# A seven-product decoder step: first quarter summed in PSUM, the last recurrent chain later, the gate product on DVE

## The chip, the cores and the metric

One core of a Trainium2 chip runs the whole program. The metric is the device time of one execution in microseconds; the median of several runs counts.

## What is computed

One layer of a hybrid decoder for a prompt of 2048 rows of 1024 numbers and 8 sample rows, in float32. Cut to what matters here:

```python
h = rmsnorm(x) * (1 + scale) + shift
q, k, v, ga, xr, gr, ma, mr = split(h @ w_in)
o  = windowed_attention(q, k, v)
ya = o * silu(ga)
xc = causal_conv(xr)                      # width 4
hs = rglru(xc)                            # h[t] = a[t] * h[t-1] + u[t]
yr = hs * silu(gr)
merged = sigmoid(ma) * (ya @ w_pa) + sigmoid(mr) * (yr @ w_pr)
y = x + gate * (merged @ w_out)
```

Beside y, the last keys, values, convolution rows and recurrent states go out.

## The kernel before

The prompt is worked in two halves of 1024 rows. Each half has its keys, values and attention first, and then a long line of 218 *slots*. A slot is twelve matmuls of 128x512 on PE: for each of four pieces of 128 rows the product of the high parts, and two with a low part (float32 is split in two fp32r numbers, "high" and "low", by a cast on ACT and a subtraction on DVE, S<-B,S or B<-B,B in the views). A matmul of this form takes about 0.23 us, a slot 2.8 us.

Most of the line is made of *Fast* units: a 256x1024 piece of an output as 2x2 quarters by seven products instead of eight (a scheme of Strassen's kind), each product one slot. Weights are loaded, added to each other and split some slots ahead. The products sum in two PSUM banks, X (tiles pg, from a pool of three) and Y (tiles pq, two). Product 0 belongs to quarter (0,0) and to all the others; so after it ACT copies bank X to SBUF (`keep`), and after product 1, which has bank Y to itself, DVE adds the two (`add`) and the quarter goes to the unit's own `evac`. Products 2 to 6 go on in the banks; two units run in turns (`pair`), so that between product 0 and product 1 of a unit there is a slot of the other unit. There are 26 Fast units per half.

What an engine does beside a slot is entered with `line.on(slot, rank, fn)`. Within a slot the ranks are issued in order: EVAC, SIDE, SPLIT, FORM, CHAIN, LATE, STORE, LOAD. Every engine works in the order of this program; nothing is reordered. All instructions carry the line of one helper (L60), so the views are read by tiles: S and B are SBUF tiles, pg, pq and pt PSUM banks, M small tiles, H middle ones, HC the state of the recurrence.

The slots of a half, in order:

- 0 to 17: first merge and attention gates.
- 18 to 129: four times `rnn(p)` (a pair of Fast units for xr and gr), each followed by a pair of gate units. The recurrent *chain* of `rnn(p)` (convolution, gate matmuls into pt, exps on ACT, a product `drive` on POOL, the scan on DVE, a product `out` on POOL, and its store) is entered at slots c(i,j). For p = 3, c(1,0) and c(1,1) are 124 and 127, so its scans stand in slots 137 and 138, its POOL products in 136 to 139.
- 130 to 157: `pa`, the attention projection, two pairs of Fast units. ACT adds 1 to the loaded merge gate (`plus`), and for three of the four quarters POOL multiplies it by the quarter (after DVE's add); the fourth is one scalar_tensor_tensor on DVE.
- 158 to 189: `pr`, the recurrent projection. Its operand is yr, which came through memory (yrd): `load_split` loads a chunk on SP, and ACT and DVE split it three slots later. In the second half eleven small stores of the final states (`state_out`, to out_dram) go through SP's queue near there.
- 190 to 217: the output projection; merged comes back from memory (mgd).

In the first half `phase_h` prepares the rows of the second one beside the pa and pr slots: loads, a root mean square per row (squares on ACT, the small M operations on POOL, the scaling on DVE), transposes on PE.

Of the kernel before, what the change touches and what calls it, by code (L numbers as in the profile page):

```python
# [16 lines left out]
ALU = mybir.AluOpType  # L17
# [24 lines left out]
def tile_hybrid_step(ctx: ExitStack, tc: tile.TileContext, x_prompt, x_sample, cache_k, cache_v, state_conv,  # L42
# [189 lines left out]
    onec = C([P, 1], tag="onec")  # L232
    V.memset(onec, 1.0)
# [186 lines left out]
    def phase_h(line, t0):  # L420

        def group(g, t0):
            xts = []
# [15 lines left out]
            for i in range(4):  # L439
                line.on(t0 + 2 * i, LOAD, lambda i=i: load(i))  # L440
                line.on(t0 + 4 + 2 * i, CHAIN, lambda i=i: rms_rows(xts[i], P))
# [608 lines left out]
    EVAC, SIDE, SPLIT, FORM, CHAIN, LATE, STORE, LOAD = range(8)  # L1050
# [83 lines left out]
    class Fast:  # L1134
# [18 lines left out]
        def mm(self, n):  # L1153
            wn, xn, bn = PROD[n]
            if n in (0, 1, 3):
                self.bank[bn] = PG() if bn == "X" else PQ()
            ps = self.bank[bn]
            for k in range(4):
                wh, wl = (t[:, k, :] for t in self.W[wn])
                xh, xl = (self.F[xn][k][:, i, :] for i in range(2))  # L1160
                T_.matmul(ps, wh, xh, start=(n in (0, 1, 3) and k == 0), stop=False, skip_group_check=True)
                T_.matmul(ps, wh, xl, start=False, stop=False, skip_group_check=True)
                T_.matmul(ps, wl, xh, start=False, stop=(k == 3), skip_group_check=True)
# [4 lines left out]
        def place(self, s):  # L1168
# [51 lines left out]
            line.on(s[0] + 1, EVAC, lambda: keep(0, 0, "X"))  # L1220
            line.on(s[1] + 1, EVAC, lambda: add(0, 0, "Y"))
# [54 lines left out]
    def stages(s, hT, hT1=None, side=None):  # L1276
# [142 lines left out]
        def rnn(p):  # L1419
# [185 lines left out]
            c = {(0, 0): t0 + 12, (0, 1): t0 + 15, (1, 0): t0 + 22, (1, 1): t0 + 25}  # L1605
# [98 lines left out]
        def pa(p):  # L1704
# [12 lines left out]
            def plus(i, j):  # L1717
                A.activation(tm[i, j], tm[i, j], AF.Identity, bias=onec)

            def evac(i, j, x, t):  # L1720
                y = tm[i, j]
                if t is None:
                    V.scalar_tensor_tensor(y, y, 1.0, x, op0=ALU.add, op1=ALU.mult)
                else:
                    G_.tensor_tensor(y, y, x, op=ALU.mult)
                    free(t)
                line.after(1 if t is None else 2, STORE, lambda: store(i, j))
# [9 lines left out]
            def loads(t0):  # L1737
                for n, i, j in ((1, 0, 0), (4, 1, 1), (5, 0, 1), (6, 1, 0)):
                    line.on(t0 + 2 * n - 4, LOAD, lambda i=i, j=j: load(i, j))
                    if n < 6:  # L1740
                        line.on(t0 + 2 * n, LATE, lambda i=i, j=j: plus(i, j))
# [11 lines left out]
        for i, (k, c) in enumerate(quarters):  # L1753
            load_split(yrd, yrx, k, c, pa_end - 9 + 7 * i // 8, 3)
# [98 lines left out]
        def out(u):  # L1853
# [12 lines left out]
            def evac(i, j, y, t):  # L1866
                if t is None:
                    t = xt[0] if end else Tt([512])
                    if end:
# [398 lines left out]
```

## Time and profile before

| | |
|---|---|
| median of three runs | 1936.6 us (1935.42 to 1936.63) |
| profiled execution | 1935.09 us, span 1933.4 us |
| PE busy | 1889.7 us, 11000 matmuls |
| DVE, ACT, POOL busy | 1421.6, 1046.9, 541.1 us |
| granted TensorE clock | 0.999 in the mean |
| line of the first half | about 297 to 962 us |
| line of the second half | about 1232 to 1926 us |

PE's busy time is modelled to the end of the pipelined matmuls; what is missing to the span is time in which PE stood. A row of a timeline gives the start in us from the span's begin, the duration, the engine and operation, how many alike follow each other, and in brackets the idle time just before and who ended it.

### The profile page before, as it was taken

How to read it: one execution, taken by the hardware profiler on the slowest of the kernel's cores; microseconds unless marked ns; L12 is line 12 of the kernel's file. 1: busy time of each engine (PE TensorE's matmuls, PEld its weight loads, DVE VectorE, ACT ScalarE, POOL GpSimd, SP SyncE). 2: the span in 40 equal slices, each digit the busy share in tenths (PEclk: the TensorE clock that was granted, in tenths of full speed). 3: DMA queues.
4: the chain of work that ended last, by engine and by line, in shares of the span. 5: the costliest groups of instructions: out<-in, count | busy, mean ns of one | idle time of the engine just before them, and what ended most of it. 6: DMA issues, size and time to landing. Idle time of an engine off the chain costs nothing. (4 is left out here: it accounts for less than half of the span.)

```text
span 1933.4 us, 31848 instructions
## 1 busy us (share of the span) xinstructions
PE 1889.7 (98%) x11000; PEld 1523.5 (79%) x11000; DVE 1421.6 (74%) x2881; ACT 1046.9 (54%) x2285; POOL 541.1 (28%) x606
## 2 busy tenths in 40 slices
PE   7999999999999999999999999999999999999999
PEld 4689887777777877787878898777888787777777
DVE  3657878578988897576735777776889798974754
ACT  4535665365757685533524566454757576942332
POOL 2224443001213222372222444400121131232711
PEclk9999999999999999999999999999999999999999
DMA  9613136445444578897822221443444455777684
GB/s 302 199 61 99 56 106 188 132 140 183 147 140 167 186 243 281 275 247 157 182 54 66 90 71 56 158 132 91 138 138 147 131 174 176 229 247 235 163 189 69
DMA packets 310912, 301.81 MB, mean 156 GB/s; under 512 B 57869, under 2 KB 220925, under 8 KB 310582
## 3 DMA queue, kind: packets, MB, share of 16 engines
q1 hardware_dynamic: 301310, 272.97, 45.4%
q0 software_dynamic: 9440, 26.80, 7.3%
q8 instruction: 87, 1.43, 0.3%
q14 instruction: 75, 0.61, 0.1%
HBM read 207.51 MB, written 102.71 MB: 160 GB/s over the span
## 5 line engine op out<-in xcount | busy, mean ns | idle before, releaser
L60 PE MATMUL pg<-S,B 128*128 128x512 f32 (+1 forms) x3840 | 917.2, 392 | 11.2 <-DVE B L60 9.3
L60 PEld LDWEIGHTS pg<-S,B 128*128 128x128 f32 (+1 forms) x3840 | 702.5, 188 | 180.2 <-DVE B L60 15.3
L60 DVE TENSOR_TENSOR B<-B,B 128x512 fp32r<-128x512 f32 (+1 forms) x756 | 565.9, 772 | 151.6 <-ACT B L60 143.5
L60 PE MATMUL pq<-S,B 128*128 128x512 f32 (+2 forms) x2208 | 482.3, 381 | 5.4 <-DVE B L60 4.9
L60 POOL TENSOR_TENSOR B<-B,B 128x512 f32<-128x512 f32 x184 | 281.7, 1553 | 717.9 <-ACT B L60 268.6
L60 PEld LDWEIGHTS pq<-S,B 128*128 128x128 f32 (+1 forms) x2208 | 369.8, 187 | 98.2 <-DVE B L60 11.5
L60 ACT CAST B<-B 128x512 fp32r<-128x512 f32 x492 | 296.3, 619 | 58.0 <-DVE B L60 33.6
L60 PE MATMUL pg<-B,S 128*128 128x256 f32 (+1 forms) x1704 | 243.8, 298 | 0.0
L60 PEld LDWEIGHTS pg<-B,S 128*128 128x128 f32 x1704 | 217.7, 189 | 17.2 <-issue 9.9
L60 DVE TENSOR_TENSOR S<-B,S 128x512 fp32r<-128x512 f32 x208 | 169.3, 835 | 31.0 <-ACT S L60 30.6
L60 ACT COPY B<-pg 128x512 f32<-128x512 f32 x118 | 69.1, 586 | 163.1 <-PE pg L60 156.7
L60 ACT CAST S<-B 128x512 fp32r<-128x512 f32 x208 | 124.5, 621 | 58.6 <-DVE B L60 20.6
L60 ACT ACTIVATE B<-B,M 128x129 f32<-128x129 f32 x260 | 102.6, 396 | 92.0 <-DVE M L60 85.5
L60 ACT ACTIVATE B<-B 128x512 f32<-128x512 f32 (+1 forms) x166 | 102.8, 629 | 87.0 <-DVE B L60 82.8
L60 POOL TENSOR_TENSOR B<-B,M 128x512 f32<-128x512 f32 x64 | 67.5, 1073 | 99.9 <-DVE M L60 99.9
L60 DVE TENSOR_TENSOR B<-pq,B 128x512 f32<-128x512 f32 x104 | 71.2, 685 | 31.9 <-PE pq L60 31.9
L60 ACT ACTIVATE B<-pg 128x512 f32<-128x512 f32 x76 | 45.1, 594 | 79.6 <-PE pg L60 78.5
L60 POOL TENSOR_TENSOR M<-M,mhalf 128x8 f32<-128x8 f32 (+4 forms) x70 | 83.8, 1197 | 5.8
L60 DVE SCALAR_TENSOR_TENSOR B<-B,VT,B 128x512 f32<-128x512 f32 x96 | 81.4, 848 | 2.3
L60 ACT COPY H<-pt 128x256 f32<-128x256 f32 (+1 forms) x51 | 17.9, 351 | 120.2 <-PE pt L60 120.2
L60 DVE SCALAR_TENSOR_TENSOR B<-B,B 128x512 f32<-128x512 f32 x106 | 78.6, 746 | 0.2
L60 POOL TENSOR_SCALAR M<-M 128x8 f32<-128x8 f32 (+5 forms) x71 | 15.6, 220 | 214.5 <-DVE M L60 208.2
(206 smaller groups left out, 1762.1 us busy)
## 6 DMA issues: line engine op xcount, KB each, us to landing
B<-in_w_in_dram SPq DMA_DIRECT2D x144, 256.0 KB
B<-yad SPq DMA_DIRECT2D x80, 256.0 KB
B<-in_w_in_dram SPq DMA_DIRECT2D x128, 128.0 KB
B<-hd SPq DMA_DIRECT2D x48, 256.0 KB
B<-in_w_out_dram SPq DMA_DIRECT2D x48, 256.0 KB
S<-in_w_ada_dram SPq DMA_DIRECT2D x32, 256.0 KB
hd<-B SPq DMA_DIRECT2D x32, 256.0 KB
yad<-S SPq DMA_DIRECT2D x16, 512.0 KB
```

Of the source, the lines that this page charges most:

```text
L60: ins = fn(*args, **kw)
```

## The change

Six edits:

1. In a Fast unit ACT copies bank X after product 0 into a new bank Y in PSUM (`onto`), one slot after product 0 at a new rank ahead of all others, and product 1 accumulates on it. DVE's `add` of the first quarter is gone; the quarter's `evac` reads the bank. That is 52 copies and 52 adds in the program; where `evac` had an SBUF tile and now has a bank, tanh reads PSUM, and 16 quarters get an ACT copy of their own.
2. In `pa` each quarter's gate product is one scalar_tensor_tensor (add 1, multiply) on DVE: 24 POOL products and 24 ACT `plus` are gone, 24 DVE operations come. The store goes one slot after the evac for all.
3. For p = 3, c(1,0) and c(1,1) are four slots later, 128 and 131, and with them the loads of the gate weights, scans (141, 142), POOL products and stores.
4. `phase_h`: the sum of squares stays where it was, the scaling comes a slot later at rank EVAC (`rms_rows` is these two in one).
5. The yrd chunks are loaded and split two slots earlier.
6. In the output projection of the second half the first quarter's sum takes the way of the others.

```diff
--- before.py
+++ after.py
@@ -229,8 +229,6 @@
     V.tensor_reduce(sel1, ident.rearrange("p (g m) -> p m g", m=32)[:, 8:9, :], op=ALU.add, axis=AX.X)
     V.tensor_tensor(sel1, sel1, ident[:, 9:10], op=ALU.add)
     V.tensor_scalar(sel1, sel1, 0.25, None, op0=ALU.mult)
-    onec = C([P, 1], tag="onec")
-    V.memset(onec, 1.0)
 
     def rstd_of(dst, ss, n, inv):
         G_.tensor_scalar(dst, ss, inv, EPS, op0=ALU.mult, op1=ALU.add)
@@ -420,7 +418,7 @@
     def phase_h(line, t0):
 
         def group(g, t0):
-            xts = []
+            xts, sums = [], {}
 
             def load(i):
                 xts.append([Tt([512]) for _ in range(2)])
@@ -438,7 +436,8 @@
 
             for i in range(4):
                 line.on(t0 + 2 * i, LOAD, lambda i=i: load(i))
-                line.on(t0 + 4 + 2 * i, CHAIN, lambda i=i: rms_rows(xts[i], P))
+                line.on(t0 + 4 + 2 * i, CHAIN, lambda i=i: sums.update({i: rms_sum(xts[i], P)}))
+                line.on(t0 + 5 + 2 * i, EVAC, lambda i=i: rms_scale(xts[i], P, sums.pop(i)))
             for f in range(KT):
                 line.on(t0 + 11 + f, SIDE, lambda f=f: turn(f))
 
@@ -1047,7 +1046,7 @@
 
 
 
-    EVAC, SIDE, SPLIT, FORM, CHAIN, LATE, STORE, LOAD = range(8)
+    ONTO, EVAC, SIDE, SPLIT, FORM, CHAIN, LATE, STORE, LOAD = range(9)
 
     class Line:
         def __init__(self):
@@ -1152,13 +1151,13 @@
 
         def mm(self, n):
             wn, xn, bn = PROD[n]
-            if n in (0, 1, 3):
+            if n in (0, 3):
                 self.bank[bn] = PG() if bn == "X" else PQ()
             ps = self.bank[bn]
             for k in range(4):
                 wh, wl = (t[:, k, :] for t in self.W[wn])
                 xh, xl = (self.F[xn][k][:, i, :] for i in range(2))
-                T_.matmul(ps, wh, xh, start=(n in (0, 1, 3) and k == 0), stop=False, skip_group_check=True)
+                T_.matmul(ps, wh, xh, start=(n in (0, 3) and k == 0), stop=False, skip_group_check=True)
                 T_.matmul(ps, wh, xl, start=False, stop=False, skip_group_check=True)
                 T_.matmul(ps, wl, xh, start=False, stop=(k == 3), skip_group_check=True)
             free(*self.W.pop(wn))
@@ -1217,8 +1216,13 @@
             def last():
                 self.evac(1, 0, bank["X"], None)
 
-            line.on(s[0] + 1, EVAC, lambda: keep(0, 0, "X"))
-            line.on(s[1] + 1, EVAC, lambda: add(0, 0, "Y"))
+            def onto():
+
+                bank["Y"] = PQ()
+                A.copy(bank["Y"], bank["X"])
+
+            line.on(s[0] + (s[1] > s[0] + 1), ONTO, onto)
+            line.on(s[1] + 1, EVAC, lambda: self.evac(0, 0, bank["Y"], None))
             line.on(s[2] + 1, EVAC, lambda: keep(0, 1, "X"))
             line.on(s[3] + 1, EVAC, lambda: keep(1, 1, "Y"))
             line.on(s[4] + 1, EVAC, lambda: add(1, 1, "X"))
@@ -1602,7 +1606,9 @@
             ux = Fast(line, F, in_cols(OFF_XR + 256 * p), xr_evac, sample(hsF, xrS[:, fsl, :], samples_conv))
             ug = Fast(line, F, in_cols(OFF_GR + 256 * p), gr_evac, sample(hsF, grS[:, fsl, :], None))
             t0 = pair(ux, ug)
-            c = {(0, 0): t0 + 12, (0, 1): t0 + 15, (1, 0): t0 + 22, (1, 1): t0 + 25}
+
+            t1 = t0 + (26 if p == 3 else 22)
+            c = {(0, 0): t0 + 12, (0, 1): t0 + 15, (1, 0): t1, (1, 1): t1 + 3}
             for i in range(2):
                 line.on(c[i, 0] - 7, LOAD, lambda i=i: gate_weights(i))
                 line.on(c[i, 0] + 1, SPLIT, lambda i=i: gate_split(i))
@@ -1714,17 +1720,12 @@
                 tm[i, j] = Tt([512])
                 ld.dma_start(tm[i, j], chunk(tmad, 2 * p + i, j))
 
-            def plus(i, j):
-                A.activation(tm[i, j], tm[i, j], AF.Identity, bias=onec)
-
             def evac(i, j, x, t):
                 y = tm[i, j]
-                if t is None:
-                    V.scalar_tensor_tensor(y, y, 1.0, x, op0=ALU.add, op1=ALU.mult)
-                else:
-                    G_.tensor_tensor(y, y, x, op=ALU.mult)
+                V.scalar_tensor_tensor(y, y, 1.0, x, op0=ALU.add, op1=ALU.mult)
+                if t is not None:
                     free(t)
-                line.after(1 if t is None else 2, STORE, lambda: store(i, j))
+                line.after(1, STORE, lambda: store(i, j))
 
             def store(i, j):
                 st.dma_start(chunk(mgd, 2 * p + i, j), tm[i, j])
@@ -1737,8 +1738,6 @@
             def loads(t0):
                 for n, i, j in ((1, 0, 0), (4, 1, 1), (5, 0, 1), (6, 1, 0)):
                     line.on(t0 + 2 * n - 4, LOAD, lambda i=i, j=j: load(i, j))
-                    if n < 6:
-                        line.on(t0 + 2 * n, LATE, lambda i=i, j=j: plus(i, j))
 
             return u, loads
 
@@ -1751,7 +1750,7 @@
         b.final = True
         pa_end = len(seq)
         for i, (k, c) in enumerate(quarters):
-            load_split(yrd, yrx, k, c, pa_end - 9 + 7 * i // 8, 3)
+            load_split(yrd, yrx, k, c, pa_end - 11 + 7 * i // 8, 3)
 
         def pr(f):
             ts = {}
@@ -1865,8 +1864,9 @@
 
             def evac(i, j, y, t):
                 if t is None:
-                    t = xt[0] if end else Tt([512])
-                    if end:
+                    plain = end and (i, j) == (1, 0)
+                    t = xt[0] if plain else Tt([512])
+                    if plain:
                         V.tensor_tensor(t, y, t, op=ALU.add)
                     else:
                         A.copy(t, y)
```

DVE in slots 137 to 140 of the first half before (pg and pq are the banks of the pa units, S and B<-B,B weight splits, HC the scans), and slots 140 to 142 after:

```order
L60 SCALAR_TENSOR_TENSOR B_7830<-B_7786,HC_125,B_7748 128x512
L60 COPY HC_125<-B_7830 128x1
L60 TENSOR_TENSOR B_8071<-B_7637,B_8070 128x512
L60 TENSOR_TENSOR S_8074<-B_7988,S_8074 128x512
L60 SCALAR_TENSOR_TENSOR B_7927<-B_7895,HC_125,B_7868 128x512
L60 COPY HC_125<-B_7927 128x1
L60 TENSOR_TENSOR B_8039<-pg_7796,B_8039 128x512
L60 TENSOR_TENSOR B_8098<-B_7677,B_8097 128x512
L60 TENSOR_TENSOR S_8101<-B_8020,S_8101 128x512
L60 TENSOR_TENSOR S_8104<-B_8022,S_8104 128x512
L60 TENSOR_TENSOR B_8068<-pg_7838,B_8068 128x512
L60 TENSOR_TENSOR B_8139<-B_7634,B_8138 128x512
```

```order
L60 TENSOR_TENSOR B_8028<-pg_7780,B_8028 128x512
L60 SCALAR_TENSOR_TENSOR B_7949<-B_7949,B_8028 128x512
L60 TENSOR_TENSOR B_8099<-B_7598,B_8098 128x512
L60 TENSOR_TENSOR S_8102<-B_8012,S_8102 128x512
L60 TENSOR_TENSOR B_7932<-pq_7951,B_7932 128x512
L60 SCALAR_TENSOR_TENSOR B_7985<-B_7985,B_7932 128x512
L60 TENSOR_TENSOR B_8134<-B_7638,B_8133 128x512
L60 SCALAR_TENSOR_TENSOR B_7913<-B_7877,HC_123,B_7846 128x512
L60 COPY HC_123<-B_7913 128x1
L60 TENSOR_TENSOR B_7964<-pq_7987,B_7964 128x512
L60 SCALAR_TENSOR_TENSOR B_8014<-B_8014,B_7964 128x512
L60 TENSOR_TENSOR B_8156<-B_8072,B_8155 128x512
```

The scans with HC stood ahead of the two pg adds; after the change they stand behind both and between the pq adds, and each of these adds is followed by a SCALAR_TENSOR_TENSOR, the gate product.

POOL over slots 131 to 145 of the first half, before and after (two operands of which the second is an evacuated quarter: a gate product):

```order
L60 TENSOR_TENSOR B_7760<-B_7760,B_7851 128x512
L60 TENSOR_TENSOR B_7794<-B_7794,B_7886 128x512
L60 TENSOR_TENSOR B_7748<-B_7748,B_7746 128x512
L60 TENSOR_TENSOR B_7868<-B_7868,B_7866 128x512
L60 TENSOR_TENSOR B_7830<-B_7830,B_7956 128x512
L60 TENSOR_TENSOR B_7960<-B_7960,B_8039 128x512
L60 TENSOR_TENSOR B_7927<-B_7927,B_7986 128x512
L60 TENSOR_TENSOR B_7990<-B_7990,B_8068 128x512
L60 TENSOR_TENSOR B_8024<-B_8024,B_7974 128x512
L60 TENSOR_TENSOR B_8054<-B_8054,B_8005 128x512
```

```order
L60 TENSOR_TENSOR B_7846<-B_7846,B_7844 128x512
L60 TENSOR_TENSOR B_7944<-B_7944,B_7942 128x512
L60 TENSOR_TENSOR B_7913<-B_7913,B_8038 128x512
L60 TENSOR_TENSOR B_8010<-B_8010,B_8068 128x512
L60 TENSOR_TENSOR M_8424<-M_8424,M_8425 128x1
L60 TENSOR_SCALAR M_8424<-M_8424 128x1
```

Before, the two drives (B_7748, B_7868) and two outs (B_7830, B_7927) of the chain stand among six gate products. After, the drives and outs stand alone, and the M operations of the normalization follow at once.

SP in the second half, around the stores of the final states (out_dram), before and after:

```order
L60 DMA mgd<-B_18843 128x512
L60 DMA B_19046<-yrd 128x512
L60 DMA out_dram<-B_19076 24x128
L60 DMA out_dram<-B_19076 8x128 x9
L60 DMA out_dram<-B_19076 64x128
L60 DMA mgd<-B_18870 128x512
L60 DMA mgd<-B_18898 128x512
L60 DMA B_19099<-yrd 128x512
L60 DMA B_19101<-tmd 128x512
L60 DMA mgd<-B_18926 128x512
L60 DMA B_19128<-yrd 128x512
```

```order
L60 DMA mgd<-B_18800 128x512
L60 DMA B_18973<-yrd 128x512
L60 DMA out_dram<-B_19003 24x128
L60 DMA out_dram<-B_19003 8x128 x9
L60 DMA out_dram<-B_19003 64x128
L60 DMA mgd<-B_18829 128x512
L60 DMA B_19025<-tmd 128x512
L60 DMA mgd<-B_18856 128x512
L60 DMA B_19052<-in_w_proj_rnn_dram 128x4x128
```

Before, two yrd loads are queued behind the eleven stores to out_dram; after, the last yrd load stands ahead of them.

## Rows read from the trace of the kernel before

**Rows 1.** the page's first part: busy us, share, instructions
```profile
PE 1889.7 (98%) x11000; PEld 1523.5 (79%) x11000; DVE 1421.6 (74%) x2881; ACT 1046.9 (54%) x2285; POOL 541.1 (28%) x606
```

**Rows 2.** what PE waited for: us in total, times, longest us
```profile
PE pg L60 <- DVE B L60: 9.3, 11, 2.1
PE pq L60 <- DVE B L60: 4.9, 7, 1.0
...
PE pg L60 <- ACT S L60: 1.6, 1, 1.6
```

**Rows 3.** stretches: length, busy us (instructions) by engine, granted clock, DMA
```profile
300.00:680.00 380.00, 377.16 (x1673) 298.80 (x1672) 311.19 (x473) 229.46 (x393) 76.23 (x55) 1.00 0.51 161
680.00:745.00 65.00, 59.68 (x247) 45.27 (x246) 64.50 (x84) 49.03 (x84) 23.51 (x14) 1.00 0.77 236
745.00:785.00 40.00, 40.00 (x173) 32.03 (x173) 29.06 (x42) 25.07 (x51) 11.65 (x13) 1.00 0.92 305
785.00:796.00 11.00, 8.93 (x35) 6.89 (x33) 9.29 (x16) 3.46 (x8) 3.30 (x7) 0.84 0.79 248
796.00:900.00 104.00, 102.47 (x472) 82.94 (x471) 70.38 (x89) 44.90 (x82) 54.51 (x54) 1.00 0.88 234
...
1638.00:1712.00 74.00, 68.90 (x405) 53.27 (x405) 72.08 (x112) 52.84 (x99) 23.76 (x14) 1.00 0.77 238
...
1760.00:1770.00 10.00, 8.05 (x33) 5.63 (x31) 3.60 (x7) 1.85 (x3) 1.74 (x2) 1.00 1.08 347
```

**Rows 4.** DVE's timeline: start, us, engine, operation, out<-in, count
```profile
729.87 0.69 DVE L60 TENSOR_TENSOR B<-B,B 128x512 fp32r<-128x512 f32 x1
...
734.77 3.49 DVE L60 TENSOR_TENSOR S<-B,S 128x512 fp32r<-128x512 f32 x2
...
742.88 1.18 DVE L60 TENSOR_TENSOR B<-B,B 128x512 fp32r<-128x512 f32 x1
```

**Rows 5.** POOL's timeline beside it
```profile
734.39 3.32 POOL L60 TENSOR_TENSOR B<-B,B 128x512 f32<-128x512 f32 x2 [2.67 <-issue]
...
741.90 1.61 POOL L60 TENSOR_TENSOR B<-B,B 128x512 f32<-128x512 f32 x1 [1.29 <-DVE B L60]
```

**Rows 6.** the page's groups: busy, mean ns, idle before
```profile
L60 ACT COPY B<-pg 128x512 f32<-128x512 f32 x118 | 69.1, 586 | 163.1 <-PE pg L60 156.7
...
L60 DVE TENSOR_TENSOR B<-pq,B 128x512 f32<-128x512 f32 x104 | 71.2, 685 | 31.9 <-PE pq L60 31.9
...
L60 DVE SCALAR_TENSOR_TENSOR B<-B,B 128x512 f32<-128x512 f32 x106 | 78.6, 746 | 0.2
```

**Rows 7.** DVE's timeline before the gap at 789
```profile
784.24 2.39 DVE L60 TENSOR_TENSOR S<-B,S 128x512 fp32r<-128x512 f32 x2
787.35 0.88 DVE L60 TENSOR_SCALAR B<-B,M 128x512 f32<-128x512 f32 x2 [0.72 <-POOL M L60]
```

**Rows 8.** POOL's timeline at that place
```profile
783.86 1.62 POOL L60 TENSOR_TENSOR B<-B,B 128x512 f32<-128x512 f32 x1 [1.29 <-ACT S L60]
```

**Rows 9.** PE's timeline behind that gap
```profile
789.49 4.14 PE L60 MATMUL pg<-S,B 128*128 128x512 f32 x10 [2.07 <-DVE B L60]
...
793.83 2.57 PE L60 MATMUL pg<-S,B 128*128 128x512 f32 x10
```

**Rows 10.** SP's timeline, second half, DMA issues
```profile
1751.09 4.03 SPq L60 DMA_DIRECT2D out_dram<-B  x11
...
1758.79 0.77 SPq L60 DMA_DIRECT2D B<-yrd  x1
```

**Rows 11.** ACT's timeline behind these loads
```profile
1765.41 0.62 ACT L60 CAST S<-B 128x512 fp32r<-128x512 f32 x1 [2.46 <-DMA B<-yrd]
```

**Rows 12.** PE's timeline behind that cast
```profile
1766.08 0.51 PE L60 MATMUL pg<-S,B 128*128 128x512 f32 x1 [1.62 <-ACT S L60]
```

**Rows 13.** ACT and PE around products 0 and 1 of one unit
```profile
887.75 0.59 ACT L60 COPY B<-pg 128x512 f32<-128x512 f32 x1 [7.00 <-PE pg L60]
...
890.34 1.32 PE L60 MATMUL pq<-S,B 128*128 128x512 f32 x5
```

## The prediction

> **What bounds the kernel now.** I read the page's busy shares first. TensorE (PE) works 1889.7 of 1933.4 us [rows 1], so the kernel is a stream of matmuls with only 43.7 us of gaps, and no edit here adds or removes a matmul. Time can only come out of those gaps, or go into new ones. The view of PE's waits then says who ends the gaps: waits for DVE's tiles B, before matmuls into pg and pq, make 14.2 us, and one of 1.6 us is for ACT's S [rows 2]. Last, the table of stretches says where they are [rows 3]. In 680 to 745 us (slots 124 to 143 of the first half) PE stands 65.0 - 59.7 = 5.3 us while DVE is busy 64.5 of 65.0: there DVE is the bound. The same slots of the second half (1638 to 1712) lose 74.0 - 68.9 = 5.1 us, with DVE at 72.1. From 785 to 796 PE stands 2.07 us and its granted clock reads 0.84 instead of 1.00. From 1760 to 1770 it stands 1.95 us. These four places hold 14.4 us. The change touches the work around each of them; elsewhere (300 to 680 for example, 2.8 us in 380) it removes DVE work ahead of gaps before which DVE was not full, and I count nothing.
>
> **Why DVE is late from 680 to 745.** In its timeline an S<-B,S or B<-B,B of 128x512 takes 0.69 us (729.87), but 3.49 for two at 734.77 and 1.18 at 742.88 [rows 4]. Both times POOL runs a 128x512 product: 3.32 us for two from 734.39, and 1.61 from 741.90 [rows 5]. So one product on POOL costs DVE 3.49 / 2 - 0.69 = 1.05 us where DVE asks just after POOL has begun, and 1.18 - 0.69 = 0.5 where it asks later. Of the six gate products on POOL in these slots I find three of the first sort and three of the second: 3 x 1.05 + 3 x 0.5 = 4.7 us of DVE's time per half.
>
> **The change, part by part.**
>
> *Gate product on DVE.* Six POOL products go in each of the two stretches: -4.7 us for DVE. Six scalar_tensor_tensor come; two of them take the place of the add of the first quarter (0.69 us, and the product is 0.75 by its group [rows 6]), so four are new: 4 x 0.75 = +3.0. Net -1.7 us of DVE work per stretch.
>
> *Last chain four slots later.* It removes nothing, but the two scans, the two products before them and the two after them (these four on POOL, at about 1.05 us of DVE each) leave slots 136 to 139, some 2 x 1.28 + 4 x 1.05 = 6.8 us of DVE's time, and land in 140 to 143. Behind those, from 745 to 785, DVE is busy 29.1 of 40.0 and PE does not stop at all [rows 3], so what is late there can be made up. (The scan's 1.28 is in order of size with two ordinary operations; I use it only for this comparison.) The convolutions and activations of that chain move from 124-127 to 128-131 likewise.
>
> Together the stretch gives back at least the net work, 1.7 us, and at most the whole gap, 5.3 (5.1 in the second half). DVE remains the fullest engine, but the work lies later, where there is room; I take the middle: **3.5 and 3.4 us**.
>
> *The gap of 789 us.* Before it DVE runs two S<-B,S in 2.39 us from 784.24, then waits 0.72 for POOL's M at 787.35 and scales for 0.88 [rows 7]. POOL was in a gate product from 783.86 for 1.62 us and could not turn to the normalization's M before [rows 8]. The weight split for PE's product comes behind that, and PE starts at 789.49 after 2.07 us [rows 9]. After the change the product is gone (2.39 - 2 x 0.69 = 1.0), the scaling is issued a slot later than its sum, behind the split (0.72 + 0.88 = 1.6), and two gate products of 0.75 come to DVE (+1.5). That is 1.1 us less just there; two earlier products of the same run of DVE work, at 1.05 each by the same price, make it 3.2, more than the 2.07. After this gap ten matmuls take 4.14 us where ten take 2.57 a little later [rows 9], which is the stretch with the granted clock of 0.84. PE had stood 2.07 us before, its longest gap here; without the gap I expect the clock to stay: 1.6 us more. **3.6 us**; between 1.1 (a shorter gap, the clock still falling) and 3.6.
>
> *The loads of yrd two slots earlier.* In the second half SP issues the last yrd load at 1758.79, behind eleven stores of the state that it could not start before 1751.09 [rows 10]. ACT's cast at 1765.41 waited 2.46 us for that load [rows 11], and PE's matmul at 1766.08 waited 1.62 us for the cast [rows 12]. Two slots are 24 matmuls, and SP's order shows both loads ahead of the eleven stores and the wait that holds them; the loads then lie more than 7 us earlier, against 1.95 us of gaps. **1.9 us**; nothing, if the load's landing is not what is late.
>
> *The first quarter in PSUM.* Now ACT copies product 0 from one bank into the next one, and product 1 waits for that copy; behind product 1 stand all of PE's matmuls, behind the copy ACT's casts of the next weights. The trace has no ACT write into PSUM. The nearest row is the copy to SBUF that it replaces, 0.586 us [rows 6]. In the tightest place that I found it starts at 887.75 and ends at 888.34, and product 1 starts at 890.34 [rows 13]: 2.0 us to spare. From below, the copy costs nothing; from above, PE waits only if it takes over 2.59 us, 4.4 times the row. I take nothing. The 28 adds that disappear with no product in their place (28 x 0.69 = 19 us of DVE) lie where DVE has room, and count for nothing as well; in the pairs of the recurrent part up to slot 123 they could take a little from the 2.8 us of 300 to 680 [rows 3]. The tanh that ACT now reads from PSUM, and sixteen more copies at 0.59, stand on an engine that is busy 49.0 of 65.0 in its fullest stretch [rows 3]; if that cover were gone, the sixteen would cost 9 us in all.
>
> **The sum.** 3.5 + 3.4 + 3.6 + 1.9 = 12.4 us. The profiled execution took 1935.1 us (span 1933.4 and 1.7 around it): 1922.7. The median of the runs is 1.5 above that execution, so 1922.7 to 1924.2; I say **1923**. Lower bounds of the four: 1.7 + 1.7 + 1.1 + 0 = 4.5, upper: 5.3 + 5.1 + 3.6 + 1.95 = 16.
>
> **Rivals.** What this kernel's runs can tell from no change is 0.2%, 3.9 us.
>
> *DVE gets work and no relief (same).* If the stretched operations at 734.77 were long for a reason of their own, taking POOL's products away frees nothing, and each stretch gets 3.0 us longer: +6.0, against -3.6 and -1.9 of the other places: about 1937. For it speaks that DVE is already full (64.5 of 65.0). Against it, every stretched operation lies beside a POOL product, and the same form takes 0.69 where POOL is idle. The Trainium skill ("Perfetto Trace Analysis", Optimizing Scalar/DVE Operations) advises that a saturated DVE may give work to ScalarE or even GpSimd, the opposite of this edit; it adds that between DVE and GpSimd this might not help, since they share a port. By the first half of that rule the time would be this rival's; the rows bear out the second half. Chance 0.09.
>
> *The gaps move (smaller gain).* DVE meets the moved chain in slots 140 to 143 together with the new products, and PE stops there; or the DMA queues, at 0.92, 0.79 and 0.88 of their time from 745 to 900 [rows 3], hand back what the first half gained. The idle share there is 40 x 0.08 + 11 x 0.21 + 104 x 0.12 = 18 us, more than the 7.1 us gained ahead of it, so only part could be lost. With half of the sum lost: 1935.1 - 6 = 1929. Chance 0.18.
>
> *All four gaps vanish* and some of 300 to 680 and 796 to 900 (2.8 and 1.5 us) with them: 1935.1 - 16 - 2 = 1917. It needs DVE never late in the stretch where it was fullest. Chance 0.12.
>
> *The copy is late (slower).* Product 1 waits in all 52 units as soon as copy and queue take more than 2.59 us after product 0; at 2.59 + 12.4 / 52 = 2.83 us it has eaten the gain, and at 3.0 it costs 52 x 0.41 = 21 us: 1944. It speaks for it that no row shows such a write and that ACT has casts in the same queue; against it stand 4.4 times the row's duration. Chance 0.06.
>
> The forecast, 1918 to 1928 on its own, has 0.55. Faster: 0.55 + 0.12 + 0.17 of the third = 0.84; same 0.10; slower 0.06. The range from 1916 to 1932 leaves out the same and slower cases and a rest at the lower end.
>
> **What would show it.** Right: from 680 to 745 and in its twin PE's gaps fall from some 5 to under 2.5 us and no S<-B,S takes 1.7 us except beside the chain's own products on POOL; the granted clock around 790 stays at 1.00; PE has no wait for ACT's S near 1766; copies pq<-pg take 0.5 to 0.7 us and PE's waits name them nowhere. Wrong: waits of PE for ACT's pq; PE waits for DVE in slots 140 to 146 as long as the old ones; gaps after 890 us that are longer by what came out before.

## The result and the profile after

The changed kernel takes 1925.8 us in the median against 1936.6: the ratio is 0.9948, with a 95% interval of 0.9936 to 0.9960, some 10 us faster (8 to 12). One execution of each kernel took several milliseconds and is left out of the ratio. A second set of runs gave 1923.8 against 1934.9, the same ratio. The trace of that second set is shown here; its execution took 1923.4 us, span 1921.7.

The page's first part and the waits of PE (a line "PE pt L60 <- DVE B L60: 3.7, 1, 3.7" is a wait of PE, before a matmul into pt, for DVE's tile B: us in total, times, longest us):

```profile
PE 1884.7 (98%) x11000; PEld 1524.7 (79%) x11000; DVE 1382.9 (72%) x2852; ACT 1038.3 (54%) x2277; POOL 498.9 (26%) x582
```

```profile
PE pg L60 <- DVE B L60: 4.5, 10, 1.1
PE pt L60 <- DVE B L60: 3.7, 1, 3.7
...
PE pg L60 <- ACT B L60: 1.2, 1, 1.2
PE pq L60 <- DVE B L60: 0.9, 2, 0.5
...
PE pt L60 <- DVE xrS L60: 0.5, 1, 0.5
```

In the kernel before, the second of these lines read:

```profile
PE pt L60 <- DVE B L60: 0.4, 1, 0.4
```

The span is 11.7 us shorter than in [rows 1]; the matmuls are the same 11000, and PE's gaps are 1921.7 - 1884.7 = 37.0 us instead of 43.7. PE's busy time itself is 5.0 us lower. The clock does not explain that, its mean is 0.998 here and was 0.999 before; the stops do in part, as shown below. Of the waits in [rows 2], the 14.2 us for DVE's B before pg and pq have become 5.4, the 1.6 us for ACT's S is gone; and one line has grown from 0.4 to 3.7 us, the wait for DVE's B before pt, in one piece.

The table of stretches (length; busy us and instructions of PE, PEld, DVE, ACT and POOL; granted clock, DMA share, GB/s). The second half starts some us earlier than before, so its rows are set to the same slots. First two rows of the kernel before, with the windows that are used from here on, then the changed kernel:

```profile
680.00:750.00 70.00, 64.68 (x269) 49.31 (x268) 69.44 (x91) 50.13 (x86) 23.72 (x14) 1.00 0.78 240
805.00:830.00 25.00, 24.51 (x121) 19.75 (x120) 12.81 (x14) 10.43 (x23) 11.59 (x17) 1.00 1.01 299
```

```profile
380.00:680.00 300.00, 296.92 (x1290) 235.40 (x1289) 245.65 (x363) 193.11 (x327) 62.08 (x45) 1.00 0.51 162
680.00:750.00 70.00, 66.75 (x285) 52.91 (x284) 65.98 (x99) 48.08 (x85) 11.39 (x8) 1.00 0.84 265
775.00:800.00 25.00, 25.00 (x120) 20.41 (x119) 14.78 (x28) 11.94 (x27) 7.73 (x14) 1.00 0.84 264
805.00:830.00 25.00, 21.32 (x99) 17.30 (x98) 12.62 (x12) 7.38 (x14) 9.65 (x13) 0.93 0.89 269
1629.00:1709.00 80.00, 78.95 (x453) 62.49 (x452) 73.58 (x129) 57.82 (x109) 11.33 (x8) 1.00 0.77 250
1744.00:1774.00 30.00, 30.00 (x158) 23.58 (x157) 11.46 (x19) 4.27 (x9) 9.46 (x9) 1.00 0.97 287
```

PE stands 3.25 us in slots 124 to 145 of the first half (70.00 - 66.75) where it stood 5.32, and 1.05 in the second half where it stood 5.10; nothing at 789, with the clock at 1.00; nothing near the yrd loads. From 380 to 680 it is 3.08 us, where it was 2.84. The row of 805 to 830 is the bad one: 3.68 us against 0.49, with a granted clock of 0.93.

A gap is not the whole price of a stop: a matmul starts every 0.23 us but is modelled to last 0.4 (398 ns in the mean for those into pg), so that a part of each stop lies under the end of the matmul ahead of it. PE's records allow another count. The same matmuls lie between two marks in both traces, so a place can be timed from the start of one matmul to the start of a later one (numbered in order of time, from 0):

| place, matmuls | before, us | after, us | difference |
|---|---|---|---|
| first stretch, 3824 to 4108 | 678.10 to 752.01 | 678.03 to 748.23 | -3.7 |
| around 789, 4229 to 4317 | 780.15 to 803.15 | 776.31 to 795.29 | -4.0 |
| around 818, 4317 to 4455 | 803.15 to 832.08 | 795.29 to 828.78 | +4.6 |
| second stretch, 9437 to 9876 | 1634.11 to 1716.02 | 1629.85 to 1707.02 | -4.7 |
| yrd loads, 10059 to 10215 | 1752.18 to 1785.05 | 1743.20 to 1773.28 | -2.8 |

The four places of the prediction give 15.3 us together, and a fifth takes 4.6 back. The rest of the trace is 1 us shorter.

In slots 140 to 143 DVE now runs like this, with POOL beside it:

```profile
729.01 2.40 DVE L60 TENSOR_TENSOR S<-B,S 128x512 fp32r<-128x512 f32 x2
...
733.05 0.68 DVE L60 TENSOR_TENSOR B<-B,B 128x512 fp32r<-128x512 f32 x1
733.65 0.68 DVE L60 TENSOR_TENSOR S<-B,S 128x512 fp32r<-128x512 f32 x1
734.25 0.68 DVE L60 TENSOR_TENSOR B<-pq,B 128x512 f32<-128x512 f32 x1
734.97 0.69 DVE L60 SCALAR_TENSOR_TENSOR B<-B,B 128x512 f32<-128x512 f32 x1
735.58 0.69 DVE L60 TENSOR_TENSOR B<-B,B 128x512 fp32r<-128x512 f32 x1
736.18 1.28 DVE L60 TENSOR_TENSOR_SCAN B<-B,HC,B 128x512 f32<-128x512 f32 x1
...
737.56 0.68 DVE L60 TENSOR_TENSOR B<-pq,B 128x512 f32<-128x512 f32 x1
738.28 1.30 DVE L60 SCALAR_TENSOR_TENSOR B<-B,B 128x512 f32<-128x512 f32 x1
```

```profile
729.39 3.19 POOL L60 TENSOR_TENSOR B<-B,B 128x512 f32<-128x512 f32 x2 [31.41 <-DMA B<-in_w_proj_attn_dram]
737.72 1.30 POOL L60 TENSOR_TENSOR B<-B,B 128x512 f32<-128x512 f32 x1 [5.14 <-DVE HC L60]
741.69 1.29 POOL L60 TENSOR_TENSOR B<-B,B 128x512 f32<-128x512 f32 x1 [2.66 <-issue]
```

Each pq quarter is followed by its gate product (0.69 us at 734.97). S<-B,S takes 0.68 us at 733.65, where [rows 4] had 3.49 for two. What is stretched now is the work beside the four chain products that POOL still has: the two S<-B,S from 729.01 take 2.40, beside POOL's from 729.39, and the gate product at 738.28 lasts 1.30, half a us more, beside POOL's from 737.72.

SP in the second half: 

```profile
1733.56 0.38 SPq L60 DMA_DIRECT2D B<-yrd  x1
1742.10 4.03 SPq L60 DMA_DIRECT2D out_dram<-B  x11
```

The last yrd load leaves at 1733.56, 8.5 us ahead of the eleven stores; in [rows 10] it came 7.7 us behind their start.

The first quarter's copy and its product 1, at the place of [rows 13]:

```profile
884.57 0.57 ACT L60 COPY pq<-pg 128x512 f32<-128x512 f32 x1 [7.05 <-PE pg L60]
...
887.14 3.40 PE L60 MATMUL pq<-S,B 128*128 128x512 f32 x14
```

```profile
L60 ACT COPY pq<-pg 128x512 f32<-128x512 f32 x52 | 29.9, 575 | 74.9 <-PE pg L60 74.9
```

The copy into PSUM takes 0.575 us in the mean of 52, as the copy to SBUF did (0.586), and product 1 starts 2.0 us after its end. PE's waits name ACT's pq nowhere.

### The profile page after: what moved, and what is told of

Its sections match the earlier page's. It is cut to its first block, busy times and chain, and to the rows that moved or that the text cites. A ratio compares the mean times of both kernels' runs of the same rounds, so it can differ in the third digit from the quotient of the medians.

```text
span 5239.5 us, 31814 instructions
## 1 busy us (share of the span) xinstructions
PE 5223.5 (100%) x11000; PEld 3200.7 (61%) x11000; DVE 1326.9 (25%) x2852; ACT 1058.2 (20%) x2277; POOL 462.6 (9%) x582
## 4 chain that ended last, share of the span: by engine, by line
PE 100%; DMA 0%; SPq 0%; issue 0%; ACT 0%; DVE 0%
PE pg L60 59%; PE pq L60 27%; PE pt L60 14%; DMA S<-in_w_ada_dram 0%; SPq L60 0%; ACT S L60 0%; DVE B L60 0%
## 5 line engine op out<-in xcount | busy, mean ns | idle before, releaser
L60 PE MATMUL pg<-S,B 128*128 128x512 f32 (+1 forms) x3840 | 2461.2, 867 | 0.0
L60 PEld LDWEIGHTS pg<-S,B 128*128 128x128 f32 (+1 forms) x3840 | 1403.3, 376 | 974.6 <-issue 958.7
L60 PE MATMUL pq<-S,B 128*128 128x512 f32 (+2 forms) x2208 | 1292.1, 833 | 0.0
L60 PEld LDWEIGHTS pq<-S,B 128*128 128x128 f32 (+1 forms) x2208 | 743.2, 381 | 521.9 <-issue 509.4
L60 DVE TENSOR_TENSOR B<-B,B 128x512 fp32r<-128x512 f32 (+1 forms) x756 | 523.2, 709 | 1432.0 <-ACT B L60 1381.8
L60 PE MATMUL pg<-B,S 128*128 128x256 f32 (+1 forms) x1704 | 708.9, 641 | 0.0
L60 PEld LDWEIGHTS pg<-B,S 128*128 128x128 f32 x1704 | 614.6, 490 | 91.5 <-issue 86.3
L60 POOL TENSOR_TENSOR B<-B,B 128x512 f32<-128x512 f32 x160 | 212.2, 1349 | 2235.0 <-ACT B L60 1173.7
L60 ACT CAST B<-B 128x512 fp32r<-128x512 f32 x492 | 296.4, 618 | 182.1 <-PE pg L60 84.9
L60 PE MATMUL pt<-ident,B 128*128 128x128 f32 (+1 forms) x480 | 186.3, 605 | 0.0
L60 DVE TENSOR_TENSOR S<-B,S 128x512 fp32r<-128x512 f32 x208 | 142.2, 701 | 105.8 <-ACT S L60 105.7
L60 ACT ACTIVATE B<-pg 128x512 f32<-128x512 f32 x76 | 45.4, 597 | 570.1 <-PE pg L60 560.2
L60 ACT CAST S<-B 128x512 fp32r<-128x512 f32 x208 | 124.7, 619 | 111.5 <-PE pg L60 80.5
L60 PEld LDWEIGHTS pt<-ident,B 128*128 128x128 f32 (+1 forms) x480 | 107.2, 228 | 56.8 <-issue 23.7
L60 PE MATMUL pt<-B,H 128*128 128x512 f32 (+1 forms) x224 | 136.8, 826 | 0.0
L60 PE MATMUL pq<-B,S 128*128 128x512 f32 x192 | 133.8, 918 | 0.0
L60 ACT COPY B<-pg 128x512 f32<-128x512 f32 x66 | 38.6, 585 | 453.3 <-PE pg L60 421.8
L60 ACT ACTIVATE B<-B 128x512 f32<-128x512 f32 x138 | 85.2, 628 | 218.1 <-DVE B L60 188.1
L60 DVE TENSOR_TENSOR B<-pt,mcT 128x512 f32<-128x512 f32 x64 | 44.3, 692 | 309.6 <-ACT B L60 273.5
L60 ACT ACTIVATE B<-B,M 128x129 f32<-128x129 f32 x260 | 102.2, 397 | 94.1 <-DVE M L60 88.3
L60 PE MATMUL pt<-B,S 128*64 128x256 f32 (+1 forms) x264 | 119.2, 960 | 0.0
L60 ACT COPY H<-pt 128x256 f32<-128x256 f32 (+1 forms) x51 | 18.0, 353 | 492.7 <-PE pt L60 492.7
```

The costliest lines, as they stand in the source:

```text
L60: ins = fn(*args, **kw)
```

## The experiments

All times are medians, and the ratio is to runs of the kernel before on the same chip. PE's gaps by place, from the tables of stretches (length less PE's busy time; 680 to 750, 775 to 800, 805 to 830, 80 us from slot 124 of the second half, 30 us around its yrd loads):

| kernel | us | ratio (95%) | 680 | 775 | 805 | second half | yrd |
|---|---|---|---|---|---|---|---|
| before | 1936.6 | 1 | 5.32 | 2.07 | 0.49 | 5.10 | 1.95 |
| a_again, the change | 1923.8 | 0.9948 (0.9935 to 0.9962) | 3.25 | 0.00 | 3.68 | 1.05 | 0.00 |
| b_gate | 1930.7 | 0.9981 (0.9972 to 0.9990) | 4.89 | 0.00 | 0.54 | 4.93 | 1.55 |
| c_onto | 1935.6 | 1.0003 (0.9995 to 1.0012) | 4.34 | 2.03 | 3.70 | 4.00 | 0.74 |
| d_chain | 1935.1 | 1.0000 (0.9991 to 1.0009) | 5.50 | 2.09 | 3.64 | 2.41 | 1.93 |
| e_yrdrms | 1933.4 | 0.9991 (0.9983 to 1.0000) | 5.31 | 0.13 | 3.68 | 4.96 | 0.00 |
| l_gatechain | 1928.0 | 0.9966 (0.9953 to 0.9978) | 2.49 | 0.00 | 3.63 | 1.44 | 1.52 |
| f_noonto | 1926.2 | 0.9954 (0.9940 to 0.9967) | 2.79 | 0.00 | 3.72 | 1.81 | 0.00 |
| g_nochain | 1930.9 | 0.9979 (0.9970 to 0.9988) | 4.12 | 0.00 | 3.62 | 3.93 | 0.00 |
| h_actscale | 1922.5 | 0.9941 (0.9928 to 0.9953) | 2.69 | 1.52 | 0.22 | 1.20 | 0.00 |
| i_actlast | 1922.1 | 0.9936 (0.9922 to 0.9950) | 3.54 | 0.00 | 0.26 | 0.98 | 0.00 |
| j_before_actlast | 1935.5 | 1.0003 (0.9995 to 1.0012) | 5.32 | 2.05 | 0.14 | 4.80 | 1.34 |
| k_copy2 | 1928.5 | 0.9963 (0.9951 to 0.9976) | 2.46 | 0.00 | 3.71 | 2.01 | 0.00 |

The lines `...` in the cuts of code below stand for lines left out.

The theory was that POOL's gate products stretch DVE in the two stretches, and that the other edits matter less; the rival that DVE gets work and no relief, so that the gain has to come from somewhere else.

**a_again** is the changed kernel itself.

> The changed kernel once more, for a trace of an undisturbed execution. Time 1924 to 1927 us, 10 to 12 us under the kernel before. By the theory of the prediction PE's gaps in slots 124 to 143 fall from 5.3 and 5.1 us to about 2 each, the 2.07 near 789 and the 1.95 near 1766 vanish; by the rival of the moved gaps some of that comes back in slots 140 to 146 or after 890 us of the first half.

Its gaps are those above: in place of 2 us each there are 3.25 and 1.05, and there is a new gap near 818, which no case of the prediction had.

**b_gate**: only the gate product on DVE.

```diff
...
-                if t is None:
-                    V.scalar_tensor_tensor(y, y, 1.0, x, op0=ALU.add, op1=ALU.mult)
-                else:
-                    G_.tensor_tensor(y, y, x, op=ALU.mult)
+                V.scalar_tensor_tensor(y, y, 1.0, x, op0=ALU.add, op1=ALU.mult)
+                if t is not None:
                     free(t)
...
```

> Of the change only the gate product as one DVE operation; quarter (0,0) still goes through the SBUF copy and the add, the chain stays. If POOL's products were what stretched DVE: 5 to 8 us faster (some 1.7 of DVE work and more of the stops in each half, most of the 3.6 at 789). Rival (DVE gets work and no relief): eight products more on DVE per half than the full change has relief for, no change or up to 4 us slower.

3.7 us faster, less than expected, and not where expected. The gap at 789 is gone, but the two stretches stay at 4.89 and 4.93. PE's timeline shows the stop, behind DVE's two scans; the ten matmuls behind it run partly at a lowered clock, 0.98 over the 70 us:

```profile
735.50 4.14 PE L60 MATMUL pq<-S,B 128*128 128x512 f32 x10 [2.08 <-DVE B L60]
```

```profile
680.00:750.00 70.00, 65.11 (x265) 49.92 (x265) 68.95 (x99) 45.71 (x79) 12.53 (x8) 0.98 0.78 246
```

DVE is busy 68.95 of the 70.00 us, where it was 69.44: what the six POOL products no longer stretch, the new operations fill. By the prediction's own prices that is 4.7 us less and 6 x 0.75 = 4.5 more, since here no add is gone; the 5 to 8 us that were expected did not follow from them.

**d_chain**: only the chain's later slots.

```diff
-            c = {(0, 0): t0 + 12, (0, 1): t0 + 15, (1, 0): t0 + 22, (1, 1): t0 + 25}
+            t1 = t0 + (26 if p == 3 else 22)
+            c = {(0, 0): t0 + 12, (0, 1): t0 + 15, (1, 0): t1, (1, 1): t1 + 3}
```

> Of the change only the last chain four slots later. Theory: it moves 6.8 us of DVE time behind slot 140 and removes none, so with the POOL products still there 0 to 3 us faster per kernel, and DVE still over 95% busy to the end of slot 143. Rival: the chain alone is what was late, 5 to 8 us faster.

No difference. In the first half the stops move along with the chain:

```profile
741.08 2.59 PE L60 MATMUL pg<-S,B 128*128 128x512 f32 x10 [0.64 <-DVE B L60]
744.20 0.70 PE L60 MATMUL pg<-S,B 128*128 128x512 f32 x2 [0.53 <-DVE B L60]
746.59 3.69 PE L60 MATMUL pg<-S,B 128*128 128x512 f32 x9 [1.69 <-DVE B L60]
```

```profile
740.95 2.31 DVE L60 TENSOR_TENSOR_SCAN B<-B,HC,B 128x512 f32<-128x512 f32 x1
...
743.98 2.56 DVE L60 TENSOR_TENSOR B<-B,B 128x512 f32<-128x512 f32 x2
```

```profile
736.67 9.33 POOL L60 TENSOR_TENSOR B<-B,B 128x512 f32<-128x512 f32 x5 [1.28 <-issue]
```

POOL is in products without a break from 736.67 to 746, the gate's and the chain's in a row, and even the scan takes 2.31 us beside them, where it takes 1.27 alone. The second half gains 2.7 us (5.10 to 2.41), and the gap in 805 to 830 takes it back.

**l_gatechain**: both edits together.

> Of the change only the gate products on DVE and the later chain. Alone they gave 3.7 us and nothing. If they need each other (the chain's DVE and POOL work finds room behind slot 140 only where the gate products no longer stretch DVE): 6 to 8 us faster than before, more than their sum. Rival: they add, 3 to 4.5 us.

6.6 us faster, against 3.7 and nothing. By the medians alone that is not clearly more than the sum, since the intervals are as wide as the difference; the traces show it. The first stretch falls to 2.49 us, where the gate products alone left 4.89 and the chain alone 5.50. In the second half it falls to 1.44, and there the chain alone had taken most of it (2.41). So in the first half neither the theory (products alone) nor its rival holds: the products must go *and* the chain must leave the slots in which the gate products now stand.

**c_onto**: only the first quarter's sum in PSUM, with what hangs on it.

```diff
...
-            line.on(s[0] + 1, EVAC, lambda: keep(0, 0, "X"))
-            line.on(s[1] + 1, EVAC, lambda: add(0, 0, "Y"))
+            def onto():
+                bank["Y"] = PQ()
+                A.copy(bank["Y"], bank["X"])
+            line.on(s[0] + (s[1] > s[0] + 1), ONTO, onto)
+            line.on(s[1] + 1, EVAC, lambda: self.evac(0, 0, bank["Y"], None))
...
```

> Of the change only the first quarter accumulated on the PSUM copy (with the evacuation that goes with it); the (0,0) gate products of pa go to DVE with it, the other gate products stay on POOL. Theory: 1 to 4 us faster, since each half has two POOL products and, in slots 124 to 143, two adds less in the bound stretch, and no PE wait for ACT's pq. Rival (late copy): slower by 5 or more with PE waits for ACT pq.

No difference in time. In its trace the two stretches and the yrd place lose 3.3 us together, and 805 to 830 gains 3.2.

**f_noonto**: the changed kernel with the SBUF copy and the add again (the reverse of that diff).

> The changed kernel with the first quarter through SBUF copy and add again. By itself the PSUM sum gave nothing measurable. If it is worth nothing in company either, this run equals the changed kernel, 1922 to 1926. Rival: with the gate products on DVE, the two adds more in slots 124 to 143 of each half are what DVE can't fit; then this is 3 to 5 us slower than the changed kernel.

0.9954 against 0.9948: the intervals lie on each other, and the gaps of the two stretches add to 4.60 against 4.30. The median is 2.4 us above that of the changed kernel, between the two cases and not clear of the noise. The sum in PSUM, the largest edit by code, gives nothing that these runs can tell; a us or two they could not tell.

**g_nochain**: the changed kernel with the chain in its old slots.

> The changed kernel with the last chain back in its four earlier slots. The run with the gate products alone had one stop of 2.1 us in slot 138 of the first half and 2.25 in the second, behind the scans. If the chain's place causes these, they come back: 3 to 5 us slower than the changed kernel. Rival: since DVE has lost two adds there, no difference.

Some 6 us slower than the changed kernel (0.9979 against 0.9948), more than the 3 to 5 expected, with gaps of 4.12 and 3.93 us in place of 3.25 and 1.05. The theory's side holds: the later chain that was worth nothing by itself carries more than half of the gain in company, most of it in the second half.

**e_yrdrms**: only the yrd loads two slots earlier and the later scaling.

```diff
...
-            load_split(yrd, yrx, k, c, pa_end - 9 + 7 * i // 8, 3)
+            load_split(yrd, yrx, k, c, pa_end - 11 + 7 * i // 8, 3)
```

> Of the change only the yrd loads two slots earlier and the scaling of the rows a slot later. Theory: the stop near 1766 goes (1.9 us); the one near 789 shrinks, since 1.6 of its DVE run moves behind the split, with the gate products still on POOL: 1 to 3.6 us. Together 3 to 5 us faster. Rival: the later scaling is given back at once in the same stretch, and only the 1.9 us of the loads show.

1.7 us, at the edge of its interval and less than the 3 to 5 expected. The yrd gap goes (1.95 to 0), and the gap at 789 falls to 0.13 although POOL's gate products are still there: these two edits are enough for it, as the gate products alone were in b_gate. Which of the two it is this run does not show, because the yrd chunks are loaded and split two slots earlier in the first half as well, around this place: SP issues the last of these loads at 791.07 in the kernel before and at 781.38 here. 3.9 us of gaps less, 3.2 given back in 805 to 830.

**k_copy2**: the copy into the second bank made twice.

```diff
-                A.copy(bank["Y"], bank["X"])
+                for _ in range(2):
+                    A.copy(bank["Y"], bank["X"])
```

> The changed kernel with the copy into the second bank made twice in a row. The trace shows 0.575 us for one and 2.0 us or more from its end to product 1; so the second costs PE nothing, and ACT 52 x 0.5 = 26 us spread over its idle time: 0 to 2 us slower than the changed kernel. Rival (late copy): ACT's queue is near the edge, PE waits for pq in many of the 52 units, 5 us or more.

0.0015 of the ratio slower than the change, some 3 us, with intervals that overlap. PE still waits for ACT's pq nowhere, so the copy itself has room to double. The added gaps are for DVE's xrS and ACT's B before pt, one of 0.7 us at 1480 and one of 1.4 at 1662. Other work in ACT's queue may be what suffers, but that is not shown: a stop of 1.5 us for ACT's B stands at the second of these places in the trace of f_noonto too, which has no such copy.

**The gap at 818.** In the changed kernel's trace DVE, POOL and PE show:

```profile
812.16 6.48 DVE L60 TENSOR_SCALAR B<-B,M 128x512 f32<-128x512 f32 x2 [2.67 <-POOL M L60]
```

```profile
812.16 6.08 DVE L60 TENSOR_SCALAR B<-B,M 128x512 f32<-128x512 f32 x1 [2.67 <-POOL M L60]
```

```profile
812.09 0.89 POOL L60 DMA_DIRECT2D mgd<-B  x1
812.75 5.20 POOL L60 TENSOR_TENSOR B<-B,B 128x512 f32<-128x512 f32 x4
```

```profile
818.30 0.33 PE L60 MATMUL pt<-ident,B 128*128 128x128 f32 x1 [3.68 <-DVE B L60]
818.38 4.58 PE L60 MATMUL pg<-S,B 128*128 128x512 f32 x12
```

The scaling of the next half's last row block is two operations, 0.88 us together elsewhere [rows 7]. Here they last 6.48, to the end of four POOL products (the scaling of the output weights); the first alone is held 6.08 us, and PE's transpose waits 3.68 us for it. The next twelve matmuls take 4.58 us instead of 3.0. In the trace of the kernel before the first takes 0.49 us, and of both together, 6.16, the second is the one that is held:

```profile
820.07 0.49 DVE L60 TENSOR_SCALAR B<-B,M 128x512 f32<-128x512 f32 x1 [3.07 <-POOL M L60]
```

```profile
820.07 6.16 DVE L60 TENSOR_SCALAR B<-B,M 128x512 f32<-128x512 f32 x2 [3.07 <-POOL M L60]
```

The transposes of the next four slots read only the first, and its gaps in 805 to 830 are 0.49 us. 8 of the 10 traces with this operation on DVE show the long gap, the kernel before and b_gate do not. In the eight POOL's first product begins 0.59 us behind the first scaling, in the two 0.63 to 0.64; what makes these hundredths of a us is not shown. The later scaling is not it, for c_onto and d_chain have the long gap without it. Nor does POOL's DMA issue hold the scaling by itself: in the kernel before, two scalings from 807.17, 0.08 us behind such an issue with no product after it, take 0.88 us together.

**h_actscale** and **i_actlast** give ACT the scaling, of all row blocks or of the last one alone:

```diff
...
+    def rms_scale_act(xs, n, ss):
+        for x in xs:
+            A.activation(x[0:n], x[0:n], AF.Identity, scale=ss[0:n, 0:1])
...
-                line.on(t0 + 5 + 2 * i, EVAC, lambda i=i: rms_scale(xts[i], P, sums.pop(i)))
+                line.on(t0 + 5 + 2 * i, EVAC, lambda i=i: (rms_scale_act if (g, i) == (1, 3) else rms_scale)(xts[i], P, sums.pop(i)))
```

> The changed kernel with the scaling of the second half's rows on ACT instead of DVE. In the trace of the changed kernel one such DVE operation of 0.44 us lasted 6.08 us beside four POOL products from 812.75 and PE stood 3.7 us at 818. If that collision is a steady part of the changed kernel: 3 to 4 us faster than it, with no PE stop near 818. Rival: the operation is blocked in some executions only, and the median moves by less than 1.5 us; or ACT's casts, now behind the scaling, cost as much.

> The changed kernel with only the very last row block of the next half (the one whose scaling lasted 6.08 us beside four POOL products) scaled on ACT. With all scalings on ACT the stop of 3.8 us at 818 went, but stops of 1.4, 0.45 and 0.4 us came at 789, 784 and 822. With one alone these should stay away: if the blocked scaling is a steady part of the changed kernel, 3 to 4 us faster than it, 1920 or so. Rival: it is blocked in some executions only, and the median gains under 2 us.

Both take the gap at 818 away (0.22 and 0.26 us). With all of them on ACT one comes at 789 in its place, behind ACT's own queue, and the median is 1.3 us below the changed kernel's, not 3 to 4:

```profile
789.12 0.33 PE L60 MATMUL pt<-ident,B 128*128 128x128 f32 x1 [1.24 <-ACT B L60]
```

i_actlast has the lowest median, 1922.1 us, 0.9936; against the change at 0.9948 that is 2.3 us, between the 3 to 4 expected and the rival's under 2, and the intervals overlap. Its trace reaches its one stop for DVE's M at 1071.1 where that of the changed kernel is at 1075.2, 4.1 us sooner, and loses 1.9 again from 1206, where the clock falls after a stop:

```profile
1205.10 0.92 PE L60 MATMUL pt<-B,hsF 128*32 128x128 f32 x16 [1.73 <-ACT S L60]
1205.95 4.33 PE L60 MATMUL pg<-S,B 128*128 128x512 f32 x12
...
1210.47 3.04 PE L60 MATMUL pg<-S,B 128*128 128x512 f32 x12
```

The same stop of 1.73 us is in the changed kernel's trace, and there the granted clock of the 16 us behind it reads 1.00 instead of 0.91. So in the traces the scaling on ACT takes the place around 818 out of the time, and in the medians it is not clear of the noise.

**j_before_actlast** does the same to the kernel before.

> The kernel before with the same last block scaled on ACT. In the one trace of before the first of the two scalings was through before POOL's products began, and PE lost only 0.65 us there. If that is how it usually goes before the change: no difference (under 1 us). Rival: the kernel before is blocked in many executions too; then it gains 2 to 4 us, and the collision is no cost of the change.

No difference, as expected. In most executions of the kernel before this place seems to cost little, as in its trace; in c_onto, d_chain and e_yrdrms it seems to cost much, since their medians come out where their gaps put them only with the 3.2 us included. Executions without a profile can't be looked into, so how often each kernel is held there stays open.

## Why the prediction was right

The time fell in the range, 1 to 3 us above the 1923 forecast, and the four places are the ones where it came from. That it fell so near is in part luck: between the same matmuls the four places gave 15.3 us where the sum had 12.4, and a place that had no term in it, the one around 818, took 4.6 back. By its steps:

- **The stretches (3.5 and 3.4 us).** Measured in gaps: 5.32 to 3.25 and 5.10 to 1.05, that is 2.1 and 4.1, 6.1 in all against 6.9; between the same matmuls 3.7 and 4.7, 8.4 in all. The sign of under 2.5 us of gaps was met in the second half alone. The sum took the length of a gap for what the gap costs, which is too little. The reason was half right. The bounds were meant as "the products' net work" for the low end and "the chain too" for the high end; b_gate and d_chain show that neither of them moves the first half's gaps by more than 0.5 us, and l_gatechain that both together take 2.8 and 3.7. I had put the chain's edit down as one that removes nothing; in company it is the larger part (without it the gaps are 0.9 and 2.9 us longer, g_nochain). What failed was to price the edits one by one where they fill the same slots. Most of the rest in the first half is at 699 and 701 (1.21 and 1.05 us), where ACT's cast and DVE's convolutions are late, not in slots 140 to 143.
- **The gap at 789 (3.6).** The gap is gone, 2.07 us. It was overdetermined: e_yrdrms and b_gate each remove it alone, and the sum of DVE's work there left out that the yrd splits of the first half move ahead as well. The 1.6 us for the clock has the right size, but was not sure to be there: behind the same gap the stretch 775 to 800 shows a granted clock of 0.93 in the kernel before and in c_onto, and 1.00 in d_chain and j_before_actlast. In d_chain ten matmuls take 2.56 us behind it, where [rows 9] had 4.14:

```profile
789.62 2.56 PE L60 MATMUL pg<-S,B 128*128 128x512 f32 x10 [2.09 <-DVE B L60]
```

- **The yrd loads (1.9).** 1.95 to 0 in gaps, 2.8 us between the same matmuls, and e_yrdrms does it alone.
- **The first quarter in PSUM (nothing).** The copy has the nearest row's duration, 0.575 for 0.586; the late copy did not come, and the 28 adds less, 38.7 us of DVE's busy time together with the other edits, count for nothing measurable (f_noonto).
- **The rivals.** "DVE gets work and no relief" was nearer to b_gate than I thought: taken alone, the gate product leaves the two stretches as they were. "The gaps move" came, but elsewhere: not in 140 to 143, and not through the DMA queues. It is the hold at 812 that in the trace took 3.2 us of gap and 1.5 of clock back, nearly a third of what the four places gave. Without it the four terms would have come out ahead: the trace is 11.7 us shorter, and i_actlast's 14.0 of span.

The mechanism behind the gain and the loss looks like one: an operation of DVE beside a POOL product. For the gain the runs show it: without the gate products on POOL, S<-B,S takes 0.68 us there. For the loss it is read from the times, the hold ends 0.3 us behind the last of the four POOL products; no run moved these products away. The Trainium skill ("SBUF — State Buffer", Who interferes with whom) says that the two share a port pair, and that of a DVE operation in a two-port mode and a POOL operation the one that issues first has the pair for its whole instruction and blocks the other fully. The long hold agrees with the blocking, 6.08 us for an operation of 0.47, and not with the rest: it lasts over four POOL products, although DVE's operation began 0.59 us ahead of the first of them. In which mode DVE worked no run here shows.

## What to carry to other kernels

Price edits that land in the same slots together: two that are worth 3.7 us and nothing alone were worth 6.6 here, and a change of place is worth something only when there is room at the new one. Where one engine has a run of operations that stretch another's, as POOL's four products do here, look at what short operation of the other may start beside it, and try that one on a third engine if PE waits for it (i_actlast). Such a place may tip over by an edit that lies ahead of it: d_chain's ends some 70 us ahead of 818 and gains nothing in the median, and its trace has the long gap. Compare the traces behind the change as well as at it, and time a place from matmul to matmul as well as by its gaps.

## What the runs showed of the hardware

- A DVE tensor_scalar of 128x512 (0.47 us) lasted 6.08 us beside four POOL tensor_tensor in a row; in 8 of 10 traces the first of two was held so, in 2 the second (5.8 us). Even a scan of 1.27 us took 2.31 beside POOL's products (d_chain), and a DVE tensor_tensor 1.7 beside one (half of 3.49, [rows 4]).
- The granted clock after a stop is not the same in all executions. Behind the 1.73 us at 1206 it read 0.91 in i_actlast and 1.00 in the changed kernel; behind the 2.0 to 2.1 us at 789, 0.93 in two traces and 1.00 in two; behind the 3.6 to 3.7 us at 818, 0.93 in seven and 1.00 in one. Such a fall costs some 1.5 us: twelve matmuls behind the stop at 818 take 4.58 us in the changed kernel and 3.03 in l_gatechain, the one trace of the eight in which the clock stayed. It can be a part of the 3 to 6 us by which executions of one kernel differ; how large a part is not shown.

```profile
817.87 3.03 PE L60 MATMUL pg<-S,B 128*128 128x512 f32 x12
```

- ACT writes a 128x512 copy into PSUM in 0.575 us, no slower than into SBUF (0.584 in the same trace).
